# Diagonal units of stick-breaking attention: a multiply-add scan over the identity in place of two masks, and half-width products in place of zero blocks

## The chip, the cores and the metric

The kernel runs on one core of a Trainium2 chip. The metric is the device time of one execution in microseconds (us). Before the change the median of three runs is 1372.65 us (1367.76 to 1372.9). The core's engines work side by side, each through its own list of instructions in order: TensorE (PE, its weight loads apart as PEld), VectorE (DVE), ScalarE (ACT), GpSimd (POOL) and SyncE (SP), which issues the DMAs.

## The reference, cut to what matters

The model is a trunk of two layers: gated linear attention, then stick-breaking attention. Only the second concerns us, and in it the 1024 prompt tokens with 16 heads of 64 columns. Key `s` is read by query `t` only if `s < t`:

```python
z = einsum('bqhd,bkhd->bhqk', q, k) * dh ** -0.5 + bias
valid = k_pos < q_pos
log_1mb = where(valid, log_sigmoid(-z), 0.0)
rest = cumsum(log_1mb, reverse=True)          # over the keys, from the last one back
a = exp(where(valid, z + rest, -inf))
out = einsum('bhqk,bkhd->bqhd', a, v)
```

In products: with beta = sigmoid(z), the weight of key `s` is beta(s) times the product of 1 - beta over the keys from `s + 1` to `t - 1`. All arithmetic is in float32 accuracy; large products use fp32r operands, each value split into a high and a low part.

## The kernel before, in words

Layer 1 works through eight head pairs `p`. For each pair TensorE multiplies the tokens, in eight blocks `t` of 128 rows and one of 64 sample rows, by 384 columns of the input projection (q, k and v; `dense`, L293), and for every two such blocks it computes 256 tokens of the gate, transposed (`dense_t`, L315). Both write tiles called `acc`, for which there are two banks of PSUM in turn (`psum` has `bufs=2`): columns of block 2m, columns of block 2m+1, gates, columns of block 2m+2, and so on. A bank is free again once its readers are done; for columns the last reader is `qk_scale` (VectorE, L810), which waits for a power that POOL computes (`qk_sums`, L804) from a sum of squares of VectorE (L802).

Between these matmuls stand the units of attention, one for each group `m` of 256 queries, each group `c <= m` of 256 keys and each head `j` of the pair. A unit goes through four steps:

- `logits`: TensorE multiplies (L881); ScalarE makes `om` = 1 - beta (L884) and `A` = beta (L885). A tile has 512 columns: two query blocks `a` of 128 rows, 256 keys each.
- `stick`: VectorE scans `om` backwards for each query block (L908) into `run`, the running product, and multiplies `A` by `run` shifted by one key (L913 or L916). `run` goes on from the unit before by way of a small copy on POOL (L903).
- `turn`: TensorE transposes `A` (L932); ScalarE and VectorE split the result into `aT`, high (L934) and low (L935).
- `weigh`: TensorE multiplies `aT` by the values (L944), four matmuls of 256 query columns: two key blocks `x`, high and low part.

A unit with `c == m` is diagonal: there are two per group and head pair, 64 in all. In it query block 0 needs only the first 128 keys, which `logits` puts last in its half so that columns 0 to 127 of the tile stay unused. The last 128 columns of both halves hold the triangle `s < t`; there POOL sets `om` to 1 and `A` to 0 where `s >= t` (two selects, L890). Key block 1 has nothing for query block 0, so POOL fills those 128 columns of both `aT` with zeros (L926), and `weigh` multiplies them along.

The order of TensorE's work is written out: every step is given a due time (`at`), and the steps are issued in the order of these times. `PACE` is 0.42 between units, `L_STICK` 0.26, `L_TURN` 0.8 and `L_AV` 1.3 later than the logits. TensorE keeps exactly that order (`manual_schedule(engines=ENGINES)`). For the other engines a scheduler picks among the instructions that it expects to be ready, so their order can differ from the text. The weights of the next pair are split beside all this: rounded on VectorE or ScalarE (L221, L219), the rest subtracted on POOL (L222). The wait on the turned keys (`qk_p`, L853 to L859) is for `tr`, which has two banks of PSUM as well.

Of the kernel before, what the change touches and what calls it, by code (L numbers as in the profile page):

```python
# [9 lines left out]
F32 = mybir.dt.float32  # L10
F32R = mybir.dt.float32r
BF = mybir.dt.bfloat16
I32 = mybir.dt.int32
AF = mybir.ActivationFunctionType
OP = mybir.AluOpType
# [61 lines left out]
def tile_hybrid_decoder(ctx, tc, x_prompt, x_sample, state_gla, cache_k, cache_v, page_table,  # L77
# [3 lines left out]
    nc = tc.nc  # L81
# [34 lines left out]
    at = line.at  # L116
# [754 lines left out]
    def logits(u, pair, p, m, c, j):  # L871
        diag = c == m
        z = bank("z")
        k = pair["k"][c][:, j].rearrange("p (s x) -> p s x", s=2)
        mm = []
        for a in range(2):
            for q in pair["q"][m]:

                mm.append((z[:, a * 256:(a + 1) * 256], q[:, j, a * 128:(a + 1) * 128], k[:, ::-1] if diag and a == 0 else k))
        for x, (out, lhs, rhs) in enumerate(mm):  # L880
            nc.tensor.matmul(out, lhs, rhs, start=x == 0, stop=x == len(mm) - 1)  # L881
        hd, v0 = 2 * p + j, 128 if diag else 0
        u["om"], u["A"] = sb("at2", "om", [128, 512], F32, 2), sb("at2", "A", [128, 512], F32, NA)
        nc.scalar.activation(u["om"][:, v0:], z[:, v0:], AF.Sigmoid, scale=-1.0, bias=K1["bias"][:, 1, hd:hd + 1])  # L884
        nc.scalar.activation(u["A"][:, v0:], z[:, v0:], AF.Sigmoid, bias=K1["bias"][:, 0, hd:hd + 1])  # L885
        if diag:

            for x, fill in ((u["om"], 1.0), (u["A"], 0.0)):
                x = x.rearrange("p (a s) -> p a s", a=2)[:, :, 128:]
                nc.gpsimd.affine_select(x, x, pattern=[[0, 2], [-1, 128]], compare_op=OP.is_gt, fill=fill,  # L890
                                        base=0, channel_multiplier=1)

    def stick(u, pair, m, c, j):
        diag = c == m
        before = pair.get("run")
        run = pair["run"] = sb("at2", "run", [128, 2, 257], F32, 2)
        ends = (128, 256) if diag else (256, 256)
        if diag:
            for a in range(2):
                nc.gpsimd.memset(run[:, a, ends[a]:ends[a] + 1], 1.0)  # L900
        else:

            nc.gpsimd.tensor_copy(run[:, :, 256:], before[:, :, 0:1])  # L903
        for a in range(2):
            n = ends[a]
            init = 1.0 if diag else before[:, a, 0:1]
            rev = u["om"][:, a * 256 + 255:(a * 256 + 255 - n) if a * 256 + 255 - n >= 0 else None:-1]
            nc.vector.tensor_tensor_scan(run[:, a, n - 1::-1], rev, rev, init,  # L908
                                         op0=OP.mult, op1=OP.bypass)
        if diag:  # L910
            for a in range(2):
                A = u["A"][:, a * 256 + 256 - ends[a]:a * 256 + 256]
                nc.vector.tensor_mul(A, A, run[:, a, 1:ends[a] + 1])  # L913
        else:
            A = u["A"].rearrange("p (a s) -> p a s", a=2)
            nc.vector.tensor_mul(A, A, run[:, :, 1:])  # L916

    def turn(u, m, c):

        diag = c == m  # L920
        tr = psum.tile([128, 4, 128], F32, name="tr")
        hi, lo = u["aT"] = [sb("at2", f"aT{x}", [128, 512], F32R, NT) for x in range(2)]
        v0 = 128 if diag else 0
        if diag:
            for x in (hi, lo):
                nc.gpsimd.memset(x[:, :128].bitcast(F32), 0.0)  # L926
        for x in range(4):
            s, a = 1 - x // 2, x % 2
            if diag and x == 0:
                continue  # L930
            col = 128 if diag and a == 0 else a * 256 + s * 128
            nc.tensor.transpose(tr[:, x], u["A"][:, col:col + 128], ident)  # L932
        tr = tr.rearrange("p a q -> p (a q)")
        nc.scalar.activation(hi[:, v0:], tr[:, v0:], AF.Copy)  # L934
        nc.vector.tensor_sub(lo[:, v0:], tr[:, v0:], hi[:, v0:])  # L935

    def weigh(u, q, pair, c, j, first, last):
        if first:
            q["po"] = bank("o").rearrange("p (j s) -> p j s", j=2)
        n = 0  # L940
        for x in range(2):
            vs = pair["v"][c][:, 1 - x, 2 * j:2 * j + 2].rearrange("p h d -> p (h d)")
            for part in u["aT"]:
                nc.tensor.matmul(q["po"][:, j], vs, part[:, x * 256:(x + 1) * 256],  # L944
                                 start=first and n == 0, stop=last and n == 3)
                n += 1

# [31 lines left out]
    def open_at2():  # L979
        opened("at2")  # L980

        K1["turn"], K1["ql"] = 0, [sb("at2", f"ql{x}", [128, 2, 256], F32R, 1) for x in range(NQ)]
        for x in K1["ql"]:
            nc.gpsimd.memset(x.bitcast(F32), 0.0)
# [4 lines left out]
    for p in range(PAIRS):  # L989
# [27 lines left out]
        for m in range(NP // 2):  # L1017
# [10 lines left out]
            for x, (j, c) in enumerate(units):  # L1028
# [3 lines left out]
                at(z0, logits, u, pair, p, m, c, j)  # L1032
                at(z0 + L_STICK, stick, u, pair, m, c, j)
                at(z0 + L_TURN, turn, u, m, c)
                at(z0 + L_AV, weigh, u, q, pair, c, j, x == 0, x == len(units) - 1)
            at(z0 + L_AV + 0.05, gate_b, q, pair, p, m)
            at(z0 + L_AV + 0.35, store_b, q, p, m)
            if p == PAIRS - 1:
# [208 lines left out]
```

## Time and profile before

| | |
|---|---|
| Profiled execution | 1375.27 us, span 1373.6 us |
| Runs | 1372.65 us median (1367.76 to 1372.9) |
| TensorE, matmuls | 1282.8 us busy (93%), 8025 of them |
| VectorE | 1012.5 us busy (74%) |
| ScalarE | 709.7 us (52%) |
| POOL | 587.0 us (43%) |
| DMA | 115.82 MB, mean 84 GB/s |
| Chain that ended last | PE 55%, DVE 18%, POOL 9%, ACT 7%, issue 7%, DMA 3% |
| Granted TensorE clock | 0.986 of full speed over the span |

Matmuls are pipelined, and their ends are modelled: a matmul's duration includes a time in which the next one already runs, so the distance from one start to the next says more than the duration. Shares over the whole span mix three stages: layer 0 (to about 530 us), layer 1 with its attention (to about 1256 us), and the rest. A wait is named by what released it last by the profile; where the named instruction had long been done, it was another.

### The profile page before, as it was taken

The page shows a single profiled execution, that of the slowest core. Times are in us where ns is not written, and L with a number is a line of the kernel's source. Part 1 is how long each engine was busy: PE and PEld are TensorE (multiplying, and loading weights), DVE is VectorE, ACT ScalarE, POOL GpSimd, SP SyncE. Part 2 cuts the span into 40 slices and gives each one's busy share as a digit, 9 for nine tenths or more (in the row PEclk, how much of TensorE's full clock was granted, in tenths as well). Part 3 has the DMA queues.
Part 4 walks back from the last instruction along what each step waited for, and adds up shares of the span by engine and source line. Part 5 has one row for each costly group of instructions (what it writes and reads, how often), then busy time and mean ns, then how long its engine had stood idle before and what let it go on. Part 6 is the DMA issues. An engine that isn't in the chain of part 4 may idle for free.

```text
span 1373.6 us, 23656 instructions
## 1 busy us (share of the span) xinstructions
PE 1282.8 (93%) x8025; PEld 1140.3 (83%) x8025; DVE 1012.5 (74%) x2047; ACT 709.7 (52%) x1640; POOL 587.0 (43%) x1101
## 2 busy tenths in 40 slices
PE   6999999999999998989989899898998989989998
PEld 5788888888878788989889898898998988877666
DVE  7858759668564457788888988789788898986443
ACT  6446245352441134566756667566666667763221
POOL 6223223223231216465655846557466574543000
PEclk9999999999999999999999999999999999999999
DMA  6311402304246423020110201102012022134762
GB/s 195 92 32 43 137 20 68 108 32 133 91 129 213 145 101 104 18 81 18 58 42 22 79 17 55 47 24 80 16 41 63 23 89 68 32 121 155 249 245 88
DMA packets 118459, 115.82 MB, mean 84 GB/s; under 512 B 11003, under 2 KB 97923, under 8 KB 118339
## 3 DMA queue, kind: packets, MB, share of 16 engines
q1 hardware_dynamic: 118338, 114.31, 27.2%
q8 instruction: 64, 1.05, 0.3%
q14 instruction: 57, 0.46, 0.1%
HBM read 83.61 MB, written 30.67 MB: 83 GB/s over the span
## 4 chain that ended last, share of the span: by engine, by line
PE 55%; DVE 18%; POOL 9%; ACT 7%; issue 7%; DMA 3%; SPq 1%; POOLq 0%; ACTq 0%; DVEq 0%
PE acc L293 31%; PE acc L315 7%; DVE run L908 4%; PE z L881 3%; PE tr L932 3%; PE o L944 2%; POOL wlo L222 2%; POOL rs L804 2%; ACT qh L853 2%; DVE whi L221 2%; PE o L544 1%; DVE aT L935 1%; DVE wr L217 1%; POOL v L819 1%; PE o L1154 1%
## 5 line engine op out<-in xcount | busy, mean ns | idle before, releaser
L293 PE MATMUL acc<-whi,h 128*128 128x512 f32 (+1 forms) x1728 | 538.7, 374 | 10.1 <-DVE qk L810 7.9
L293 PEld LDWEIGHTS acc<-whi,h 128*128 128x128 f32 x1728 | 313.5, 189 | 41.1 <-ACT sh L954 4.2
L293 PE MATMUL acc<-wlo,h 128*128 128x512 f32 (+1 forms) x864 | 322.5, 373 | 3.9 <-DVE wlo L222 2.5
L315 PE MATMUL acc<-h,whi 128*128 128x256 f32 (+5 forms) x832 | 193.5, 318 | 10.3 <-DVE g L512 5.1
L222 POOL TENSOR_TENSOR wlo<-wr,whi 128x512 fp32r<-128x512 f32 x98 | 139.1, 1422 | 123.5 <-DVE whi L221 93.2
L293 PEld LDWEIGHTS acc<-wlo,h 128*128 128x128 f32 x864 | 162.8, 188 | 22.7 <-DVE wlo L222 3.2
L908 DVE TENSOR_TENSOR_SCAN run<-om,run 128x256 f32<-128x256 f32 x192 | 146.7, 802 | 11.0 <-ACT om L884 10.5
L315 PEld LDWEIGHTS acc<-h,whi 128*128 128x128 f32 (+2 forms) x832 | 141.3, 189 | 15.1 <-DVE g L512 6.0
L934 ACT ACTIVATE aT<-tr 128x512 fp32r<-128x512 f32 (+1 forms) x160 | 88.9, 556 | 103.9 <-PE tr L932 90.2
L884 ACT ACTIVATE om<-z,bias 128x512 f32<-128x512 f32 (+1 forms) x160 | 103.3, 646 | 52.6 <-PE z L881 43.1
L932 PE MATMUL tr<-ident,A 128*128 128x128 f32 x576 | 91.5, 277 | 39.3 <-POOL v L819 18.3
L315 PE MATMUL acc<-h,wlo 128*128 128x256 f32 (+2 forms) x392 | 123.8, 316 | 0.5 <-POOL wlo L222 0.5
L293 PE MATMUL acc<-w,h 128*128 128x384 f32 (+1 forms) x480 | 122.6, 365 | 0.7 <-DVE qk L810 0.7
L932 PEld LDWEIGHTS tr<-ident,A 128*128 128x128 f32 x576 | 69.5, 142 | 55.1 <-POOL run L903 19.4
L935 DVE TENSOR_TENSOR aT<-tr,aT 128x512 fp32r<-128x512 f32 (+1 forms) x160 | 100.8, 630 | 9.1 <-ACT aT L934 6.8
L944 PE MATMUL o<-aT,v 128*128 128x256 f32 x640 | 105.0, 286 | 0.0
L885 ACT ACTIVATE A<-z,bias 128x512 f32<-128x512 f32 (+1 forms) x160 | 102.4, 640 | 0.0
L944 PEld LDWEIGHTS o<-aT,v 128*128 128x128 f32 x640 | 97.2, 194 | 1.8 <-DVE aT L935 1.1
L908 DVE TENSOR_TENSOR_SCAN run<-om 128x128 f32<-128x128 f32 (+1 forms) x128 | 85.0, 695 | 13.6 <-POOL om L890 13.6
L881 PE MATMUL z<-kc,qh 128*128 128x256 f32 x320 | 86.1, 290 | 7.3 <-DVE kc L858 7.3
L804 POOL TENSOR_TENSOR rs<-ms,half_exp 128x4 f32<-128x4 f32 (+1 forms) x72 | 83.9, 1166 | 20.3 <-DVE ms L802 18.8
L293 PEld LDWEIGHTS acc<-w,h 128*128 128x128 f32 x480 | 82.2, 189 | 7.2 <-issue 2.5
(274 smaller groups left out, 2531.7 us busy)
## 6 DMA issues: line engine op xcount, KB each, us to landing
wr<-in_w_in_b_dram SPq DMA_DIRECT2D x64, 256.0 KB, 3.0
wr<-in_w_in_a_dram SPq DMA_DIRECT2D x32, 256.0 KB, 3.2
kp<-in_cache_k_dram SPq DMA_DIRECT2D x16, 512.0 KB, 5.0
vp<-in_cache_v_dram SPq DMA_DIRECT2D x16, 512.0 KB, 4.5
o_d<-og SPq DMA_DIRECT2D x60, 128.0 KB, 1.8
x<-in_x_prompt_dram SPq DMA_DIRECT2D x8, 512.0 KB, 4.8
wr<-in_w_in_a_dram SPq DMA_DIRECT2D x32, 128.0 KB, 3.7
n<-in_state_gla_dram SPq DMA_DIRECT2D x8, 512.0 KB, 3.9
```

The source lines that it names most:

```text
L222: engine.tensor_sub(e.lo[:, :m], raw[:, :m], e.hi[:, :m])
L293: nc.tensor.matmul(st["ps"][:x.shape[1], :n], x, (w[k].hi if part == 0 else w[k].lo)[:, :n], start=first, stop=last)
L315: nc.tensor.matmul(st[key][:x.shape[1], :n], x, y, start=first, stop=last)
L804: nc.gpsimd.tensor_tensor(st["rs"][:n], ms[:n], half_exp[:n], op=OP.pow)
L881: nc.tensor.matmul(out, lhs, rhs, start=x == 0, stop=x == len(mm) - 1)
L884: nc.scalar.activation(u["om"][:, v0:], z[:, v0:], AF.Sigmoid, scale=-1.0, bias=K1["bias"][:, 1, hd:hd + 1])
L885: nc.scalar.activation(u["A"][:, v0:], z[:, v0:], AF.Sigmoid, bias=K1["bias"][:, 0, hd:hd + 1])
L908: nc.vector.tensor_tensor_scan(run[:, a, n - 1::-1], rev, rev, init, op0=OP.mult, op1=OP.bypass)
L932: nc.tensor.transpose(tr[:, x], u["A"][:, col:col + 128], ident)
L934: nc.scalar.activation(hi[:, v0:], tr[:, v0:], AF.Copy)
L935: nc.vector.tensor_sub(lo[:, v0:], tr[:, v0:], hi[:, v0:])
L944: nc.tensor.matmul(q["po"][:, j], vs, part[:, x * 256:(x + 1) * 256], start=first and n == 0, stop=last and n == 3)
```

## The change

Three edits, all in diagonal units.

The masks go. The scan of a diagonal unit becomes state = om(s) x state + eye(s), from zero, where `eye` is 128 columns of zeros and the identity, built once when the attention opens. For `s > t` the state stays 0, at `s = t` it becomes 1, and from there it is the running product. `A` times the shifted `run` is then 0 for `s >= t` without a mask on `A`, and the first value of `run` is set to 0 in place of 1.

The zero blocks go. `weigh` multiplies key block 1 of a diagonal unit for the last 128 query columns alone, in matmuls of 128 columns in place of 256, and takes that block second, so that the first matmul of a group still writes the whole width.

The two memsets of `aT` go with them.

```diff
@@ -883,12 +883,6 @@
         u["om"], u["A"] = sb("at2", "om", [128, 512], F32, 2), sb("at2", "A", [128, 512], F32, NA)
         nc.scalar.activation(u["om"][:, v0:], z[:, v0:], AF.Sigmoid, scale=-1.0, bias=K1["bias"][:, 1, hd:hd + 1])
         nc.scalar.activation(u["A"][:, v0:], z[:, v0:], AF.Sigmoid, bias=K1["bias"][:, 0, hd:hd + 1])
-        if diag:
-
-            for x, fill in ((u["om"], 1.0), (u["A"], 0.0)):
-                x = x.rearrange("p (a s) -> p a s", a=2)[:, :, 128:]
-                nc.gpsimd.affine_select(x, x, pattern=[[0, 2], [-1, 128]], compare_op=OP.is_gt, fill=fill,
-                                        base=0, channel_multiplier=1)
 
     def stick(u, pair, m, c, j):
         diag = c == m
@@ -896,17 +890,22 @@
         run = pair["run"] = sb("at2", "run", [128, 2, 257], F32, 2)
         ends = (128, 256) if diag else (256, 256)
         if diag:
+
+
             for a in range(2):
-                nc.gpsimd.memset(run[:, a, ends[a]:ends[a] + 1], 1.0)
+                nc.gpsimd.memset(run[:, a, ends[a]:ends[a] + 1], 0.0)
         else:
 
             nc.gpsimd.tensor_copy(run[:, :, 256:], before[:, :, 0:1])
         for a in range(2):
             n = ends[a]
-            init = 1.0 if diag else before[:, a, 0:1]
             rev = u["om"][:, a * 256 + 255:(a * 256 + 255 - n) if a * 256 + 255 - n >= 0 else None:-1]
-            nc.vector.tensor_tensor_scan(run[:, a, n - 1::-1], rev, rev, init,
-                                         op0=OP.mult, op1=OP.bypass)
+            if diag:
+                nc.vector.tensor_tensor_scan(run[:, a, n - 1::-1], rev, K1["eye"][:, 255:(255 - n) if n < 256 else None:-1],
+                                             0.0, op0=OP.mult, op1=OP.add)
+            else:
+                nc.vector.tensor_tensor_scan(run[:, a, n - 1::-1], rev, rev, before[:, a, 0:1],
+                                             op0=OP.mult, op1=OP.bypass)
         if diag:
             for a in range(2):
                 A = u["A"][:, a * 256 + 256 - ends[a]:a * 256 + 256]
@@ -921,9 +920,6 @@
         tr = psum.tile([128, 4, 128], F32, name="tr")
         hi, lo = u["aT"] = [sb("at2", f"aT{x}", [128, 512], F32R, NT) for x in range(2)]
         v0 = 128 if diag else 0
-        if diag:
-            for x in (hi, lo):
-                nc.gpsimd.memset(x[:, :128].bitcast(F32), 0.0)
         for x in range(4):
             s, a = 1 - x // 2, x % 2
             if diag and x == 0:
@@ -934,14 +930,16 @@
         nc.scalar.activation(hi[:, v0:], tr[:, v0:], AF.Copy)
         nc.vector.tensor_sub(lo[:, v0:], tr[:, v0:], hi[:, v0:])
 
-    def weigh(u, q, pair, c, j, first, last):
+    def weigh(u, q, pair, m, c, j, first, last):
         if first:
             q["po"] = bank("o").rearrange("p (j s) -> p j s", j=2)
         n = 0
-        for x in range(2):
+        for x in (1, 0):
+
+            q0 = 128 if c == m and x == 0 else 0
             vs = pair["v"][c][:, 1 - x, 2 * j:2 * j + 2].rearrange("p h d -> p (h d)")
             for part in u["aT"]:
-                nc.tensor.matmul(q["po"][:, j], vs, part[:, x * 256:(x + 1) * 256],
+                nc.tensor.matmul(q["po"][:, j, q0:], vs, part[:, x * 256 + q0:(x + 1) * 256],
                                  start=first and n == 0, stop=last and n == 3)
                 n += 1
 
@@ -979,6 +977,9 @@
     def open_at2():
         opened("at2")
 
+        eye = K1["eye"] = sb("at2", "eye", [128, 256], BF, 1)
+        nc.gpsimd.memset(eye[:, :128], 0.0)
+        nc.gpsimd.tensor_copy(eye[:, 128:], identb)
         K1["turn"], K1["ql"] = 0, [sb("at2", f"ql{x}", [128, 2, 256], F32R, 1) for x in range(NQ)]
         for x in K1["ql"]:
             nc.gpsimd.memset(x.bitcast(F32), 0.0)
@@ -1032,7 +1033,7 @@
                 at(z0, logits, u, pair, p, m, c, j)
                 at(z0 + L_STICK, stick, u, pair, m, c, j)
                 at(z0 + L_TURN, turn, u, m, c)
-                at(z0 + L_AV, weigh, u, q, pair, c, j, x == 0, x == len(units) - 1)
+                at(z0 + L_AV, weigh, u, q, pair, m, c, j, x == 0, x == len(units) - 1)
             at(z0 + L_AV + 0.05, gate_b, q, pair, p, m)
             at(z0 + L_AV + 0.35, store_b, q, p, m)
             if p == PAIRS - 1:
```

The scheduler's order for ScalarE stays what it was, but for one exchange of two instructions; TensorE's is the same but for the widths. VectorE's and POOL's change. In the rows of the order, a scan is named SCALAR_TENSOR_TENSOR, a name ends in a buffer's number where one is left, and line numbers after the change are lower by a few: L904 and L907 are the scans of diagonal and other units, L912 and L915 the products (L913 and L916 before), L931 the subtraction (L935 before), L899 the copy (L903 before), L942 `weigh` (L944 before).

VectorE, third head pair, from the scaling of the sample rows on. Before:

```order
L810 TENSOR_TENSOR qk<-xr,rs_9122 64x256
L935 TENSOR_TENSOR aT_9200<-tr,aT_9199 128x512
L810 TENSOR_TENSOR qk<-acc,rs_9195 128x256
L935 TENSOR_TENSOR aT_9248<-tr,aT_9247 128x512
L908 SCALAR_TENSOR_TENSOR run<-om 128x128
L908 SCALAR_TENSOR_TENSOR run<-om 128x256
L913 TENSOR_TENSOR A<-A,run 128x128
L908 SCALAR_TENSOR_TENSOR run<-om,run 128x256
L913 TENSOR_TENSOR A<-A,run 128x256
L908 SCALAR_TENSOR_TENSOR run<-om,run 128x256
L802 TENSOR_REDUCE ms_9286<-sq 128x4
L916 TENSOR_TENSOR A<-A,run 128x512
```

The same place after the change:

```order
L810 TENSOR_TENSOR qk<-xr,rs_8995 64x256
L931 TENSOR_TENSOR aT_9071<-tr,aT_9070 128x512
L904 SCALAR_TENSOR_TENSOR run<-om,eye 128x128
L904 SCALAR_TENSOR_TENSOR run<-om,eye 128x256
L912 TENSOR_TENSOR A<-A,run 128x128
L912 TENSOR_TENSOR A<-A,run 128x256
L810 TENSOR_TENSOR qk<-acc,rs_9066 128x256
L931 TENSOR_TENSOR aT_9115<-tr,aT_9114 128x512
L907 SCALAR_TENSOR_TENSOR run<-om,run 128x256 x2
L915 TENSOR_TENSOR A<-A,run 128x512
L802 TENSOR_REDUCE ms_9153<-sq 128x4
```

The diagonal unit's four instructions have moved ahead of the scaling (L810) and of the second subtraction, and the next unit's scans behind all of these; the sum of squares (L802) has moved behind the next unit's product.

POOL, the same place, before:

```order
L804 TENSOR_TENSOR rs_9195<-ms_9190,half_exp 128x4
L812 TENSOR_TENSOR kout<-qk,kn 64x128
L222 TENSOR_TENSOR w_9098<-wr,w_9097 128x512
L890 AFFINE_SELECT om<-om 128x2x128
L890 AFFINE_SELECT A<-A 128x2x128
L820 TENSOR_TENSOR v_9276<-v,v_9276 128x128
L812 TENSOR_TENSOR kout<-qk,kn 128x128
L926 MEMSET aT_9305 128x128
L926 MEMSET aT_9306 128x128
L903 COPY run<-run 128x2
```

POOL after the change:

```order
L804 TENSOR_TENSOR rs_9066<-ms_9061,half_exp 128x4
L812 TENSOR_TENSOR kout<-qk,kn 64x128
L222 TENSOR_TENSOR w_8971<-wr,w_8970 128x512
L820 TENSOR_TENSOR v_9143<-v,v_9143 128x128
L899 COPY run<-run 128x2
L812 TENSOR_TENSOR kout<-qk,kn 128x128
```

The selects and memsets are gone; the copy of `run` has moved ahead of the product for the output (`kout`), which waits for L810.

VectorE, seventh head pair, after its diagonal scans, before:

```order
L913 TENSOR_TENSOR A<-A,run 128x128
L913 TENSOR_TENSOR A<-A,run 128x256
L908 SCALAR_TENSOR_TENSOR run<-om,run 128x256 x2
L802 TENSOR_REDUCE ms_14176<-sq 128x4
L916 TENSOR_TENSOR A<-A,run 128x512
L975 TENSOR_TENSOR h_81<-xr,h_80 128x2x256
L935 TENSOR_TENSOR aT_14196<-tr,aT_14195 128x384
L908 SCALAR_TENSOR_TENSOR run<-om,run 128x256 x2
L810 TENSOR_TENSOR qk<-acc,rs_14181 128x256
```

VectorE there after the change:

```order
L907 SCALAR_TENSOR_TENSOR run<-om,run 128x256 x2
L915 TENSOR_TENSOR A<-A,run 128x512
L802 TENSOR_REDUCE ms_13851<-sq 128x4
L973 TENSOR_TENSOR h_81<-xr,h_80 128x2x256
L931 TENSOR_TENSOR aT_13871<-tr,aT_13870 128x384
L810 TENSOR_TENSOR qk<-acc,rs_13856 128x256
L907 SCALAR_TENSOR_TENSOR run<-om,run 128x256 x2
```

The scaling (L810) has moved from behind to ahead of the last two scans.

## Rows read from the trace of the kernel before

**Rows 1.** Busy us by stretch: span, PE, PEld, DVE, ACT, POOL, PEclk, DMA, GB/s

```profile
604.00:616.00 12.00, 8.96 (x50) 8.50 (x49) 8.88 (x19) 4.06 (x9) 7.79 (x15) 0.72 0.16 44
720.00:800.00 80.00, 73.52 (x504) 70.44 (x503) 67.64 (x130) 53.85 (x116) 49.22 (x100) 0.98 0.16 46
780.00:790.00 10.00, 6.93 (x44) 6.47 (x43) 8.39 (x16) 3.71 (x9) 7.13 (x14) 0.83 0.18 49
1129.00:1140.00 11.00, 7.67 (x58) 7.03 (x57) 10.63 (x20) 6.42 (x14) 7.67 (x14) 1.00 0.28 86
```

**Rows 2.** Waits, 530 to 1256 us: who <- releaser: us, times, longest

```profile
PEld tr L932 <- POOL run L903: 19.4, 6, 3.2
...
PE tr L932 <- DVE kc L859: 11.9, 8, 1.8
...
PE acc L293 <- DVE qk L810: 8.6, 10, 1.7
...
PEld tr L932 <- POOL v L819: 1.8, 1, 1.8
```

**Rows 3.** Timeline, 776 to 789 us: start, us, engine, line, operation [idle before]

```profile
775.55 0.60 ACT L885 ACTIVATE A<-z,bias 128x384 f32<-128x384 f32 x1
...
777.42 0.67 DVE L935 TENSOR_TENSOR aT<-tr,aT 128x512 fp32r<-128x512 f32 x1
...
778.66 0.42 DVE L810 TENSOR_TENSOR qk<-acc,rs 128x256 f32<-128x256 f32 x1 [0.56 <-POOL rs L804]
...
779.00 1.28 POOL L222 TENSOR_TENSOR w<-wr,w 128x512 fp32r<-128x512 f32 x1
...
779.65 0.87 PE L315 MATMUL acc<-h,w 128*128 128x256 f32 x6
...
780.24 0.41 POOL L890 TENSOR_SCALAR_AFFINE_SELECT om<-om 128x256 f32<-128x256 f32 x1
...
780.68 1.47 DVE L908 TENSOR_TENSOR_SCAN run<-om 128x128 f32<-128x128 f32 x2 [1.01 <-POOL om L890]
...
782.08 0.47 DVE L913 TENSOR_TENSOR A<-A,run 128x128 f32<-128x128 f32 x1
...
782.47 0.77 DVE L908 TENSOR_TENSOR_SCAN run<-om,run 128x256 f32<-128x256 f32 x1
...
783.17 0.39 DVE L913 TENSOR_TENSOR A<-A,run 128x256 f32<-128x256 f32 x1
...
783.71 0.52 PE L932 MATMUL tr<-ident,A 128*128 128x128 f32 x3 [3.07 <-POOL v L819]
...
785.45 1.00 POOL L804 TENSOR_TENSOR rs<-ms,half_exp 128x4 f32<-128x4 f32 x1
...
788.54 0.52 PE L293 MATMUL acc<-w,h 128*128 128x384 f32 x2
```

**Rows 4.** Groups by form on POOL: busy us, mean ns of one | idle before

```profile
L890 POOL TENSOR_SCALAR_AFFINE_SELECT om<-om 128x256 f32<-128x256 f32 x64 | 28.2, 441 | 42.2 <-ACT om L884 42.2
```

**Rows 5.** Timeline of DVE, 711 to 713 us, a diagonal unit without subtraction beside it

```profile
711.41 1.00 DVE L908 TENSOR_TENSOR_SCAN run<-om 128x128 f32<-128x128 f32 x2
...
712.64 0.62 DVE L913 TENSOR_TENSOR A<-A,run 128x128 f32<-128x128 f32 x2
```

**Rows 6.** Timeline, 763 to 767 us, a diagonal unit beside POOL's subtraction

```profile
763.30 1.28 POOL L222 TENSOR_TENSOR wlo<-wr,whi 128x512 fp32r<-128x512 f32 x1
763.59 2.02 DVE L908 TENSOR_TENSOR_SCAN run<-om 128x128 f32<-128x128 f32 x2
```

**Rows 7.** Groups by form on DVE: layer 0's scan, multiply then add

```profile
L465 DVE TENSOR_TENSOR_SCAN t<-rst,xb 128x384 f32<-128x384 bf16 x8 | 7.5, 933 | 0.0
```

**Rows 8.** Timeline of PE, 800 to 812 us: four products of one unit

```profile
803.05 0.63 PE L944 MATMUL o<-aT,v 128*128 128x256 f32 x4
```

**Rows 9.** Groups by form on PEld: weight loads of 128 and of 32 columns

```profile
L944 PEld LDWEIGHTS o<-aT,v 128*128 128x128 f32 x640 | 97.2, 194 | 1.8 <-DVE aT L935 1.1
...
L1154 PEld LDWEIGHTS o<-vp,aTs 128*32 128x32 f32 x128 | 3.4, 115 | 4.3 <-issue 2.0 <-ACT As L1130 0.6 <-ACT oms L1129 0.4
```

## The prediction

> **What bounds the kernel now.** I began with the busy time by stretch [rows 1]. In a typical 80 us of layer 1's attention TensorE is busy 73.5 us and VectorE 67.6: TensorE sets the pace, and VectorE is close enough behind that what TensorE still loses is likely to be a wait on it. The waits of that stage [rows 2] agree: the largest single entry is six waits of 3.2 us in front of the transposes of L932, 19.4 us together; then come waits on the turned keys (L859), and on the scaling of q and k (L810) that frees an `acc` bank. Third, the order of time around one of the six [rows 3]. The reader is to see this: the sigmoids of the diagonal unit were done at 776.1, but POOL got to the select on `om` only at 780.24, behind a weight subtraction (L222), and VectorE's scans began at 780.68. VectorE had meanwhile run L810 (778.66) and another unit's subtraction, had stood idle for 1.0 us, and had the next unit's scan (782.47) between the two products. The last product ended at 783.56; the transposes started 0.15 us later, at 783.71, some 3.2 us after TensorE was ready for them (780.5). The page names POOL tiles as releasers, but those ended earlier; VectorE's L913 came last. Fourth, the clock [rows 1]: in the stretch of such a wait the granted clock is 0.83 of full speed (0.72 where the low stretch is longer), that is, some microseconds at 1.2 in place of 2.4 GHz, right after TensorE stood still. A wait of 1.8 us in the seventh pair ([rows 2], between 1129 and 1140) left the clock at 1.00.
>
> **The change, part by part.** There are 64 diagonal units, eight to a head pair.
>
> *POOL.* 128 selects go, and 128 memsets of 128 columns. The selects on `om` take 28.2 us and have 42.2 us of idle POOL ahead of them [rows 4]; those on `A` are as many and as large. POOL is not the bound, so this is worth only what it uncovers below. Added are one memset and one copy for the identity, beside dense work ahead of the attention: nothing.
>
> *The scan.* Multiply-add in place of multiply alone, with a second tensor. The trace has multiply-add scans over a bf16 and an fp32 operand: 933 ns for 384 columns [rows 7], 2.4 ns a column. The present diagonal scans, 128 and 256 columns with nothing beside them, take 1.00 us together [rows 5], 2.6 ns a column. So I take no difference. Bounds: 0.1 us less a unit, by the straight ratio; above, a second tensor could cost as much again, 1 us a unit (rival three).
>
> *Contention.* Scans beside POOL's weight subtraction took 2.02 us [rows 6] against 1.00 [rows 5]: 1.0 us more for one subtraction. The selects go, the subtractions stay.
> By the Trainium skill, "GPSIMD Engine Reference", section "Key points", POOL shares its memory interfaces with VectorE and contends with instructions that have two SBUF inputs. The two rows agree. If that gain fell on the path in all 64 units at the 1.0 us of the row, it would be 64 us; a select is shorter than a subtraction, most units have slack, and I count none of it by itself.
>
> *The order.* TensorE's order is as before but for widths. VectorE's isn't: in the block above the two scans and both products now stand together, straight behind the subtraction of 777.42, and L810 and the other subtraction behind them. Worked through with [rows 3]: the subtraction ends at 778.09; scans 1.00, products 0.62 [rows 5], and 1.0 for the L222 that starts at 779.00: `A` is ready at 780.7. L810 (0.42) ends at 781.1. That is the catch: `acc` has two banks, and the gate columns of L315, which start at 779.65, take the bank that L810 frees (it ended at 779.08, 0.57 before). With a hop of 0.15, as between 783.56 and 783.71, they now start at 781.25: a new wait of 1.6 us. The transposes stand 0.85 behind (779.65 to 780.5), so they start at 782.1 in place of 783.71: 1.6 us gained of 3.2.
>
> *What is late next.* The following L810 frees the bank of the next columns (788.54). Before it now stand a subtraction, two scans, a product and a reduction, about 0.67 + 1.5 + 0.7 + 0.4, so POOL's power (1.0) begins at 784.4 and L810 ends at 785.8, with the hop 785.95. TensorE needs 8.9 us from L315 to there, less 3.2 of wait and 1.7 of clock: it is ready at 785.25 and waits 0.7.
>
> *The clock.* (1 - 0.72) x 12 = 3.4 us, and (1 - 0.83) x 10 = 1.7. Of the six stretches two are like the first and four like the second: 13.6 us, of which about 1.1 fell on the wait itself. If 1.6 and 0.7 us apart do to the clock what 1.8 did in the seventh pair, nothing, 12.5 us come back. Bounds: 0 and 12.5.
>
> *Other waits.* L810's own, 8.6 us in ten [rows 2]: in the seventh pair L810 moves ahead of two scans; a third, 2.9. The eight on L859, 11.9 us: VectorE gets there sooner without selects beside its scans, but the subtractions stay; a fifth, 2.4. Bounds of the two together: 1 us lost in each of the eight pairs where the order goes wrong, 8, and all of the 20.5 gained.
>
> *Narrower products.* 128 matmuls go from 256 to 128 columns. Four of 256 follow each other 0.117 us apart (0.63 less the 0.28 of the last, over three) [rows 8]. Each loads its own 128 weight columns: 194 ns against 115 for 32 [rows 9], 0.82 ns a column, 105 ns for 128. I take 0.108 a matmul: 128 x 0.009 = 1.1 us. Bounds: half of 0.117, 7.5 us gained; and, as no row has fp32r under 256 columns, 0.1 us lost each, 12.8.
> The Trainium skill's "TensorE: Matmul & The Clock Gate", section "LDWEIGHTS (loading the stationary operand)", gives P/1.2 ns for P columns, 107 ns for 128: a rule against the gain. The slope of [rows 9] agrees. By it the sum has an estimate of 1.3 us here; by streaming alone, 7.5.
>
> **Sum.** Six blocks: 6 x (1.6 - 0.7) = 5.4, and 12.5 of clock. With 2.9, 2.4 and 1.1: 24.3 us. The profiled execution took 1375.3 (span 1373.6); the median of the runs is 1372.65, 2.6 lower. 1372.65 - 24.3 = 1348.4: I forecast 1348.
>
> **Rivals.**
> 1. *The bank hides* (more gain). If L222 falls elsewhere, `A` is ready at 779.7, L810 ends at 780.1, the new wait is 0.6 and the next one nil. For: POOL has less ahead of L222. Against: L222 waits for its own weights. 6 x 2.6 + 12.5 + 6.4 = 34.5: 1338.
> 2. *The wait only changes its name* (less gain). Two L222 beside the scans put L810 another 1.0 us later; 2.6 and 0.7 us of standing still bring the clock down as 3.2 did. For: [rows 6]. The six blocks then give 6 x (0.6 - 0.7), nearly nothing, and the clock nothing; 6 is left: 1367.
> 3. *The scan pays for its second operand* (slower). Twice the time is 1 us a unit, 64 in all; VectorE, at 67.6 of 80, goes over TensorE's 73.5 and becomes the bound. If three quarters land on the path, 1348 + 48 = 1396. It decides from 24 us on the path, 0.5 us a unit at that share. Against: [rows 7].
> 4. *Narrow fp32r matmuls are slow.* +12.8 on an engine that is the bound: 1361. No row speaks for it.
> 5. *It does not do what it says.* The zero columns are replaced by less work, not left for others: the order shows 128 matmuls of half width and no select in attention. I give this no chance of its own.
>
> **How the numbers follow.** Forecast 0.62, rival 1 0.13, rival 2 0.15, rival 3 0.05, rival 4 0.05. The forecast's own range is 1341 to 1357. The range of 8 in 10 takes in rivals 1 and 4, and reaches towards rival 2: 1336 to 1365. A measurement of this kernel can tell about 0.5% (7 us) from no change. The forecast, rivals 1 and 4 and a third of 2 are faster by that: 0.85; the rest of rival 2 is the same: 0.10; rival 3 is slower: 0.05.
>
> **What would show it.** Right: the 3.2 us waits at the diagonal transposes are gone, L315 waits about 1.6 us for L810 in the same six blocks, and the granted clock there is 1.00. Diagonal scans keep 1.0 us where nothing runs beside them. Narrow matmuls stand about 0.11 us apart. Wrong: clock stretches of 0.8 remain; L315's wait is over 2.5 us; scans of 256 columns over 0.8 us with POOL idle; or 0.2 us between narrow matmuls.

## The result and the profile after

The changed kernel takes 1355.18 us (1352.66 to 1355.67) against 1372.35: a ratio of 0.9884, 95% interval 0.9863 to 0.9904, or 17.2 us. A second timing, beside the first experiments, gave 1352.29 against 1371.44, 0.9859 (0.9842 to 0.9877). The forecast was 1348, with a range of 1336 to 1365. The profiled execution took 1355.22 (span 1353.5), 20.05 less than that of before.

Busy time by stretch, with the columns of [rows 1]: a typical 80 us of attention, the stretch that answers to the first of [rows 1], and one in the second head pair. The 80 us of [rows 1] were another part of attention, so the first line compares with them only roughly.

```profile
560.00:640.00 80.00, 75.06 (x524) 71.39 (x523) 68.20 (x130) 53.46 (x113) 40.57 (x69) 1.00 0.16 45
601.00:613.00 12.00, 10.06 (x72) 9.08 (x72) 11.21 (x20) 5.88 (x13) 9.65 (x14) 1.00 0.30 85
...
676.00:688.00 12.00, 9.55 (x54) 9.23 (x54) 11.39 (x20) 9.01 (x19) 8.37 (x11) 0.86 0.38 112
```

PE comes from 73.5 to 75.1 of 80 us, POOL falls from 49.2 to 40.6, and VectorE hardly moves. Where the granted clock was 0.72 it is 1.00. One low stretch has come up elsewhere, 0.86 at 676; another, at 1206, stood in the trace of before as well, at 1225.

TensorE's waits from 530 to 1240 us: who, for whom, us, times, longest.

```profile
PE acc L315 <- DVE qk L810: 9.0, 6, 1.7
PE tr L928 <- DVE kc L859: 8.3, 6, 2.4
...
PE acc L293 <- DVE qk L810: 7.1, 14, 1.2
...
PE tr L928 <- ACT A L885: 2.4, 2, 1.2
```

The six waits of 3.2 us [rows 2] are gone. L315's wait for L810, the new one of the forecast, is now the largest entry: 1.7 us in five blocks and 0.4 in the seventh pair. The last line is no new wait: it holds two of the eight that [rows 2] puts down to L859, at the same transposes. The block of [rows 3] in order of time:

```profile
772.02 1.38 POOL L804 TENSOR_TENSOR rs<-ms,half_exp 128x4 f32<-128x4 f32 x1
...
772.43 1.02 DVE L904 TENSOR_TENSOR_SCAN run<-om,eye 128x128 f32<-128x128 f32 x2
...
773.38 2.09 DVE L912 TENSOR_TENSOR A<-A,run 128x128 f32<-128x128 f32 x2
...
773.92 1.26 POOL L222 TENSOR_TENSOR w<-wr,w 128x512 fp32r<-128x512 f32 x1
...
775.39 0.41 DVE L810 TENSOR_TENSOR qk<-acc,rs 128x256 f32<-128x256 f32 x1
...
775.95 0.96 PE L315 MATMUL acc<-h,w 128*128 128x256 f32 x6 [1.72 <-DVE qk L810]
...
776.86 0.49 PE L928 MATMUL tr<-ident,A 128*128 128x128 f32 x3
...
779.98 0.42 DVE L810 TENSOR_TENSOR qk<-acc,rs 128x256 f32<-128x256 f32 x1 [0.65 <-POOL rs L804]
...
780.55 0.59 PE L293 MATMUL acc<-w,h 128*128 128x384 f32 x2 [0.23 <-DVE qk L810]
```

The scans now run early, 1.02 us, as [rows 5] had them; POOL's power (L804) stands beside them, but no subtraction. The two products, however, take 2.09, against 0.62 there: POOL's subtraction runs beside them. L810 stands behind the products and ends 0.15 before L315 starts. The transposes no longer wait at all, and the next L810 costs L293 0.23.

### The profile page after: what moved, and what is told of

Same layout as the page of the kernel before. It is cut to its first block, busy times and chain, and to the rows that moved or that the text cites. A ratio compares the mean times of both kernels' runs of the same rounds, so it can differ in the third digit from the quotient of the medians.

```text
span 1353.5 us, 23356 instructions
## 1 busy us (share of the span) xinstructions
PE 1274.4 (94%) x8025; PEld 1129.1 (83%) x8025; DVE 1008.2 (74%) x2047; ACT 708.9 (52%) x1640; POOL 516.0 (38%) x847
## 4 chain that ended last, share of the span: by engine, by line
PE 56%; DVE 23%; ACT 7%; issue 5%; POOL 4%; DMA 3%; SPq 1%; DVEq 0%; POOLq 0%; ACTq 0%
PE acc L293 33%; PE acc L315 6%; PE z L881 3%; DVE run L907 3%; PE tr L928 3%; PE o L942 2%; DVE aT L931 2%; ACT qh L853 2%; DVE whi L221 2%; POOL rs L804 2%; DVE qk L810 1%; DVE A L915 1%; DVE run L904 1%; DVE A L912 1%; PE o L544 1%
## 5 line engine op out<-in xcount | busy, mean ns | idle before, releaser
L293 PE MATMUL acc<-whi,h 128*128 128x512 f32 (+1 forms) x1728 | 540.9, 375 | 9.4 <-DVE qk L810 6.3
L293 PEld LDWEIGHTS acc<-whi,h 128*128 128x128 f32 x1728 | 313.8, 189 | 41.3 <-ACT sh L952 3.7
L293 PE MATMUL acc<-wlo,h 128*128 128x512 f32 (+1 forms) x864 | 322.9, 374 | 3.9 <-DVE wlo L222 2.6
L315 PE MATMUL acc<-h,whi 128*128 128x256 f32 (+5 forms) x832 | 191.4, 316 | 17.6 <-DVE qk L810 7.3
L222 POOL TENSOR_TENSOR wlo<-wr,whi 128x512 fp32r<-128x512 f32 x98 | 144.5, 1479 | 128.6 <-DVE whi L221 94.5
L293 PEld LDWEIGHTS acc<-wlo,h 128*128 128x128 f32 x864 | 163.1, 189 | 22.2 <-DVE wlo L222 3.2
L315 PEld LDWEIGHTS acc<-h,whi 128*128 128x128 f32 (+2 forms) x832 | 137.7, 185 | 24.4 <-issue 8.9
L907 DVE TENSOR_TENSOR_SCAN run<-om,run 128x256 f32<-128x256 f32 x192 | 142.9, 785 | 15.7 <-ACT om L884 15.1
L293 PE MATMUL acc<-w,h 128*128 128x384 f32 (+1 forms) x480 | 123.1, 366 | 0.8 <-DVE qk L810 0.8
L315 PE MATMUL acc<-h,wlo 128*128 128x256 f32 (+2 forms) x392 | 122.2, 312 | 0.3 <-POOL wlo L222 0.3
L931 DVE TENSOR_TENSOR aT<-tr,aT 128x512 fp32r<-128x512 f32 (+1 forms) x160 | 100.9, 630 | 11.1 <-ACT aT L930 8.8
L885 ACT ACTIVATE A<-z,bias 128x512 f32<-128x512 f32 (+1 forms) x160 | 102.4, 640 | 0.0
L942 PE MATMUL o<-aT,v 128*128 128x256 f32 (+1 forms) x640 | 98.8, 276 | 0.0
L942 PEld LDWEIGHTS o<-aT,v 128*128 128x128 f32 x640 | 95.2, 190 | 1.7 <-DVE aT L931 0.9
L804 POOL TENSOR_TENSOR rs<-ms,half_exp 128x4 f32<-128x4 f32 (+1 forms) x72 | 87.6, 1217 | 21.3 <-DVE ms L802 18.9
L293 PEld LDWEIGHTS acc<-w,h 128*128 128x128 f32 x480 | 82.2, 189 | 7.6 <-issue 2.9
L899 POOL COPY run<-run 128x2 f32<-128x2 f32 x96 | 32.7, 341 | 135.9 <-DVE run L907 77.5
```

The source lines that it names most:

```text
L222: engine.tensor_sub(e.lo[:, :m], raw[:, :m], e.hi[:, :m])
L293: nc.tensor.matmul(st["ps"][:x.shape[1], :n], x, (w[k].hi if part == 0 else w[k].lo)[:, :n], start=first, stop=last)
L315: nc.tensor.matmul(st[key][:x.shape[1], :n], x, y, start=first, stop=last)
L804: nc.gpsimd.tensor_tensor(st["rs"][:n], ms[:n], half_exp[:n], op=OP.pow)
L942: nc.tensor.matmul(q["po"][:, j, q0:], vs, part[:, x * 256 + q0:(x + 1) * 256], start=first and n == 0, stop=last and n == 3)
```

## The experiments

The runs stand in three sets, each timed beside the kernel before, which took 1371.44 us in the first set (the changed kernel, full width, the other sequence, the products behind L810), 1371.32 in the second (narrow products alone, idle work, the two with subtractions on VectorE) and 1372.51 in the third (no selects, six of eight on VectorE). The changed kernel itself stands only in the first, so across sets the ratios to the kernel before are compared.

> The changed kernel itself, beside the three variants of it, so that they are compared on one chip: 1355 us, with at most one low stretch of the clock inside attention.

Measured: 1352.29, ratio 0.9859, with one low stretch inside attention, again at 679.

### Which part of the change does it

First the kernel before without its selects. It leaves out the diagonal masks, and nothing stands in for them.

```diff
-            for x, fill in ((u["om"], 1.0), (u["A"], 0.0)):
-                nc.gpsimd.affine_select(...)
```

> The kernel before without its 128 selects; the diagonal masks are left out, the scans are of one tensor, the zero blocks and the full width stay. Theory A (all of the gain is the selects' going, the multiply-add scan costs nothing): 1352.5, as the changed kernel with full width, with 1.9 us in front of L315 in place of the six waits of 3.2 and no low clock there. Theory B (the second tensor costs up to 0.1 us a scan, 64 units on the path in part): 1348 to 1350. Theory C (the new scan gave part of the gain): over 1356.

Measured: 1353.96, ratio 0.9870 (0.9850 to 0.9889), against 0.9859 and 0.9884 of the changed kernel. Theory A: the selects' going gives the whole gain, as far as some 4 us of uncertainty let one tell. But VectorE's order in this run is, instruction for instruction, that of the changed kernel. So the run prices the selects together with the order that their absence brings, and doesn't part the two. In the old order of [rows 3] the scans could have started without the selects at 779.7, where VectorE fell idle, in place of 780.68: an estimate of 1.0 us for the selects by themselves. Nor was it tried to keep the selects and to move the subtraction that stands ahead of them on POOL. The largest wait is that of the changed kernel:

```profile
PE acc L315 <- DVE qk L810: 9.0, 6, 1.7
```

Then the change without the narrow products (`q0 = 0`, and the zero blocks back).

> The changed kernel with the products of the diagonal units at full width again, zero blocks and their 128 memsets on POOL included; VectorE's and ScalarE's order stay word for word. Theory A (the trace after: the second narrow product of a pair follows the first by 58 ns, and what comes next follows it by 110, in place of 117 and 118): 64 x 0.067 = 4.3 us come back, 1359.5. Theory B (the prediction: a product is bound by the load of its own weights, 0.009 us each): 1.1 us come back, 1356.3. Rival C: the memsets on POOL delay other work on the path: over 1362.

Measured: 1352.53, 0.24 more than the changed kernel. C falls. The 4.3 us of A lie at the edge of what two medians of four can tell (1350.0 to 1354.5 and 1349.5 to 1355.7), and the 1.1 of B below it, so the spacing has to decide. For theory A I had read only the products themselves. TensorE in the same unit of both, the changed kernel first, then full width:

```profile
837.78 0.57 PE L942 MATMUL o<-aT,v 128*128 128x256 f32 x4
838.19 0.39 PE L293 MATMUL acc<-whi,hs 128*128 128x384 f32 x1
838.41 0.33 PE L293 MATMUL acc<-wlo,hs 128*64 128x384 f32 x1
```

```profile
839.19 0.63 PE L944 MATMUL o<-aT,v 128*128 128x256 f32 x4
839.66 0.33 PE L293 MATMUL acc<-whi,hs 128*128 128x384 f32 x1
839.83 0.33 PE L293 MATMUL acc<-wlo,hs 128*64 128x384 f32 x1
```

The four products take 0.41 in place of 0.47 us, but the second matmul after them starts 0.22 behind the first in place of 0.17: from the first product to there it is 0.63 and 0.64. Over all 64 units 58 and 8 ns are saved at the pair and 55 are paid there: some 11 ns a unit, 0.7 us in all. A falls. A third run asks whether equal weights have a part in it.

```diff
-        for x in (1, 0):
-            for part in u["aT"]:
+        for part in u["aT"]:
+            for x in (1, 0):
```

> The changed kernel with the four products of a unit in another sequence: both blocks of the high part, then both of the low part, so that no two that follow each other have the same weights. The same products, the same widths. Theory A (58 ns apart only because the second of a pair has the weights of the first, whose load needs no wait): about 110 ns behind each narrow product, 64 x 0.052 = 3.3 us lost, 1358.5. Theory B (a narrow product takes 58 ns whatever its weights, and only the one after it waits): the narrow ones again 58 in front of what follows, or the sum of the four as in the changed kernel: 1355.

Measured: 1353.96, ratio 0.9872 (0.9856 to 0.9888), 1.7 us above the changed kernel, which two medians of four can't tell from nothing, nor from the 3.3 of theory A. The trace decides: each narrow product is followed after 58 ns by one with other weights, and the next but one comes after 170 in place of 117; the four take 407 ns (404 before). Theory A, which had 110 ns there, falls: the saving is paid back two matmuls later, whatever the weights.

And the narrow products alone, on the kernel before:

> The kernel before with only the narrow products: selects and scans as they were, no zero blocks. Its VectorE order has L810 two places earlier in six blocks. Theory (from the runs so far: 67 ns saved at the pair, 55 paid back by the second product after it, so 11 ns a unit): 0.7 us, 1371, with the six waits of 3.2 us and the low clock behind them as before. Rival (the zero blocks' memsets delay the selects on POOL): the six waits shrink below 2.5 us, 1360.

Measured: 1376.51, ratio 1.0039 (1.0020 to 1.0058): slower, and neither theory had it. The waits in front of the transposes grew from 3.1 to 3.4 us in five of six blocks, and the low clock behind them is of the long kind, 0.72 in 12 us, again in five of six blocks (one of them here, then the wait), where two had it before:

```profile
782.00:794.00 12.00, 8.61 (x48) 8.15 (x47) 9.89 (x19) 3.81 (x9) 6.79 (x12) 0.72 0.14 41
```

```profile
PE tr L929 <- DVE A L913: 21.5, 7, 3.4
```

VectorE's order moved in six places here (the L810 behind the transposes two earlier), so this run does not price the products. The longer wait arises ahead of that place. In the block of [rows 3], VectorE, then POOL:

```profile
784.13 0.90 DVE L908 TENSOR_TENSOR_SCAN run<-om,run 128x256 f32<-128x256 f32 x1
784.95 0.60 DVE L913 TENSOR_TENSOR A<-A,run 128x256 f32<-128x256 f32 x1
```

```profile
784.56 0.71 POOL L820 TENSOR_TENSOR v<-v,v 128x128 fp32r<-128x128 f32 x1
```

With the memsets gone, another subtraction of POOL (L820) comes up beside this scan and the last product. They take 0.90 and 0.60, against 0.77 and 0.39 in [rows 3], some 0.3 us together, as much as the wait has grown. That this is the cause is read from the trace, not tested, and why the clock stayed low longer was not isolated.

### The clock by itself

```diff
+        for x in range(fill):        # 16 in the six blocks
+            nc.tensor.transpose(tr[:, 0], ident, ident)
```

> The kernel before with 16 more transposes of the identity on TensorE in front of the transposes of the diagonal unit in the six blocks with a 3.2 us wait, into the block of the tr tile that nobody reads: 1.75 us of work in place of standing still, which takes nothing off the end of the wait. Theory A (the low clock follows the standing still, and about 11 of the 17 us gained are clock): the six low stretches go, 1372 - 11 = 1361, with the last transposes as late as before. Theory B (the clock falls for another reason, or the gain is all in the waits): 1372, low stretches as before.

Measured: 1362.08, ratio 0.9935 (0.9915 to 0.9955): 9.2 us gained by giving TensorE idle work. Here too the L810 behind the transposes moved a few places in the six blocks, as the addition shifts the schedule, so a small part of the 9.2 may be the order's. The block of [rows 3], and its stretch:

```profile
775.57 1.91 PE L924 MATMUL tr<-ident 128*128 128x128 f32 x16
778.79 0.52 PE L934 MATMUL tr<-ident,A 128*128 128x128 f32 x3 [1.31 <-POOL v L819]
```

```profile
772.00:784.00 12.00, 10.69 (x84) 10.07 (x83) 9.11 (x18) 4.94 (x10) 9.43 (x18) 1.00 0.23 64
```

The transposes start 3.3 us after the last matmul of the gates in front of them (775.45 to 778.79), as before, but only 1.3 of that is standing still, and the clock stays at 1.00 through all of attention. Theory A: in these blocks the low clock goes when the standing still does.

### What holds up L810

One rule for VectorE's order puts the products behind L810 in those blocks.

```diff
+                        tc.add_manual_dep(x.ins, K1["scaled"].ins.name, ...)   # product after L810
```

> The changed kernel with one rule for VectorE's order, in seven blocks (the last head pair has none): the products of the diagonal unit at the gates come behind L810, the scans stay ahead of it. Theory A (the 1.88 us in front of L315 are the wait for the bank that L810 frees; rs is there at 604.01 and the scans end at 604.06): L315's wait falls to under 0.3 us, the transposes of the diagonal unit wait about 1.0 in its place, 0.85 us gained in each of the five or six blocks that had it: 1350.5. Theory B (the wait only moves, since the products are late by as much): 1355, with waits of some 1.8 us at the transposes. Slower, if L810 has to stand idle for rs in other blocks: 1358.

Measured: 1354.37, ratio 0.9878 (0.9861 to 0.9894): nothing gained. VectorE, then POOL, then TensorE, in the first block:

```profile
603.14 0.42 DVE L810 TENSOR_TENSOR qk<-acc,rs 128x256 f32<-128x256 f32 x1
603.48 2.23 DVE L915 TENSOR_TENSOR A<-A,run 128x128 f32<-128x128 f32 x2
```

```profile
603.50 1.29 POOL L222 TENSOR_TENSOR wlo<-wr,whi 128x512 fp32r<-128x512 f32 x1
```

```profile
605.86 0.52 PE L938 MATMUL tr<-ident,A 128*128 128x128 f32 x3 [1.08 <-DVE A L915]
```

L315 no longer waits, so L810 was indeed what freed its bank. But the products, still beside the subtraction, take 2.23, the transposes wait 1.08, as theory A had it, and the next L293 waits 1.1 for its own L810, which it had left out. By the time it is theory B: the wait has moved. So the subtraction is moved instead, one a block:

```diff
+        if n in range(85, 126, 8):   # on VectorE, behind L810
+            x = nc.vector.tensor_sub(e.lo[:, :m], raw[:, :m], e.hi[:, :m])
```

> The changed kernel, with one weight subtraction (L222) a block moved from POOL to VectorE, straight behind L810, in the six blocks where it ran beside the products of the diagonal unit; VectorE's order is otherwise word for word the same. Theory A (the products take 2.1 us in place of 0.62 because of that subtraction, and with that L810 and the bank are late): products 0.62, L810 1.4 us earlier, L315's wait from 1.88 to about 0.4, some 1.5 us gained in each of five or six blocks: 1344 to 1345. Theory B (L810 waits for rs, or VectorE's 0.69 us more are lost again): 1351 to 1353.

Measured: 1346.88, ratio 0.9818 (0.9795 to 0.9841), against 0.9859 of the changed kernel: some 5.5 us less, give or take 4.

```profile
603.26 0.86 DVE L921 TENSOR_TENSOR A<-A,run 128x128 f32<-128x128 f32 x2
604.04 0.41 DVE L817 TENSOR_TENSOR qk<-acc,rs 128x256 f32<-128x256 f32 x1
604.37 0.68 DVE L224 TENSOR_TENSOR wlo<-wr,whi 128x512 fp32r<-128x512 f32 x1
```

```profile
604.60 0.47 PE L322 MATMUL acc<-h,whi 128*128 128x256 f32 x2 [0.47 <-DVE qk L817]
...
609.80 0.41 PE L300 MATMUL acc<-whi,h 128*128 128x384 f32 x1 [0.83 <-DVE qk L817]
```

The products are down from 2.09 to 0.86, by as much as the subtraction takes on POOL, and L315's wait (L322 here) from 1.7 to 0.47; 0.6 of the 1.25 goes to the next L810. So the mechanism was that of theory A, but not its sum. From start to start of TensorE, between this trace and that of the changed kernel in the first set, 5.5 us are gained in front of L315 and 3.4 lost in front of L293, 2.1 in all. Another 2.8 come from the second pair, where a wait of 2.4 us and the low clock behind it are gone; they are gone in the run with the products behind L810 too, which moved no subtraction. What happens there stands under *The clock* below. Then all 64 of them (`engine` is VectorE there):

> The changed kernel with all 64 weight subtractions of the attention stage on VectorE in place of POOL. Theory A (a subtraction beside VectorE's scans and products holds them up by 1.0 to 1.5 us, more than the 0.69 us that it takes on VectorE): waits shrink in most blocks, 1342 to 1350. Theory B (VectorE, 74% busy, takes 44 us more and becomes the bound, since most subtractions now run beside PSUM reads that they do not hold up): 1360 to 1375.

Measured: 1346.16, ratio 0.9815 (0.9792 to 0.9837): inside the times of theory A, but no different from the run before it (1343.3 to 1346.9 here, 1343.9 to 1348.3 there). The other 58 subtractions bring nothing more that the times can tell. Attention in the changed kernel and in this one:

```profile
560.00:1240.00 680.00, 637.68 (x4374) 603.51 (x4373) 589.92 (x1127) 454.32 (x962) 337.43 (x573) 1.00 0.18 55
```

```profile
560.00:1240.00 680.00, 640.70 (x4414) 606.24 (x4413) 590.24 (x1198) 456.45 (x967) 265.47 (x511) 1.00 0.19 58
```

In the same 680 us VectorE does 71 instructions more, 64 of them these subtractions, in the same busy time, 590 us: what it takes over is paid for by what no longer holds it up. L315's wait for L810 is gone. But a new wait has come: two subtractions now stand together in front of one product.

```profile
PE tr L928 <- DVE A L915: 13.0, 8, 2.2
```

The last of this line puts those two back on POOL.

> The run before it with the subtractions on VectorE, but the two of each head pair that stood together on VectorE in front of a product (1.4 to 1.7 us of new wait in seven pairs) back on POOL: six of eight a pair on VectorE. Theory A (the new wait was VectorE's own 1.26 us for those two): the new wait goes and the rest stays, 1346 - 8 = 1338. Theory B (on POOL the two hold up the scan and the product beside them by as much, as they did in the changed kernel): the wait there is again that of the changed kernel, 1342 to 1346.

Measured: 1361.7, ratio 0.9920 (0.9899 to 0.9940). Both theories missed. The order changed with the engines: the second L810 of a block is now behind two scans, and in three blocks L293 waits 1.9 to 2.0 for it. The wait that was to go has grown, from 13.0 to 15.0 us, and the low clock is back four times, each time right behind one of these waits (1.9, 2.0, 1.9 and 2.3 us at 856, 942, 1028 and 1202). That the order is the cause was not tested by itself.

```profile
PE acc L293 <- DVE qk L810: 15.0, 16, 2.0
PE tr L928 <- DVE A L915: 15.0, 8, 2.3
```

## Why the prediction was right, and where its sizes were off

Direction, range and mechanism held; the gain was over-sized, 24.3 forecast and 17.2 measured. TensorE's 8025 matmuls stand in the same order in both traces, so the difference can be worked out start by start. In the six blocks the intervals in front of L315, of the transposes and of the next L293 are counted. Elsewhere in attention an interval counts as a wait where TensorE stood idle before the matmul in one of the traces, else as clock where the granted clock was low, else as narrower products from the first product of a diagonal unit to the second matmul behind its four:

| us | forecast | between the two profiles |
|---|---|---|
| waits of the six blocks | 5.4 | 8.1 |
| clock | 12.5 | 9.4 |
| other waits (L810, L859) | 5.3 | 4.5 |
| narrower products | 1.1 | 0.6 |
| rest of attention | 0 | -1.8 |
| outside attention | 0 | -0.7 |
| sum | 24.3 | 20.05 |

*Six blocks.* The transposes gained 19.3 us, L315 lost 9.4, together 9.9 against the 9.6 of six times 1.6; the next L293 lost 1.8 in place of six times 0.7. The new wait of 1.6 us at L315 came as 1.7 in five blocks, the 0.7 at the next L293 as 0.2 to 0.6. That the 1.6 came out so well is partly luck: the 1.0 us of POOL's subtraction was put on the scans. They kept 1.02, and the products took it, with 1.5. The price of 1.0 was itself read too simply: beside the scans of [rows 6] there stood a select on `A` (764.53) and the start of another L222 (765.04) as well.

*The clock.* Of the terms, this step was the most over-sized. "12.5 us come back" took the upper bound itself. The low stretches of the six blocks did return 10.9, but a new one took 1.5. It came in the second head pair, where the two scans of another diagonal unit met two subtractions in a row and its second product a third (POOL, VectorE, then TensorE):

```profile
672.96 1.27 POOL L222 TENSOR_TENSOR wlo<-wr,whi 128x512 fp32r<-128x512 f32 x1 [0.42 <-DVE whi L221]
674.18 1.41 POOL L222 TENSOR_TENSOR w<-wr,w 128x512 fp32r<-128x512 f32 x1
...
676.35 1.29 POOL L222 TENSOR_TENSOR w<-wr,w 128x512 fp32r<-128x512 f32 x1
```

```profile
672.73 0.68 DVE L931 TENSOR_TENSOR aT<-tr,aT 128x512 fp32r<-128x512 f32 x1
673.34 2.81 DVE L904 TENSOR_TENSOR_SCAN run<-om,eye 128x128 f32<-128x128 f32 x2
...
676.60 1.32 DVE L912 TENSOR_TENSOR A<-A,run 128x256 f32<-128x256 f32 x1 [0.28 <-POOL run L899]
```

```profile
679.83 0.52 PE L928 MATMUL tr<-ident,A 128*128 128x128 f32 x3 [2.45 <-DVE kc L859]
```

The scans take 2.81 us, the second product starts 0.28 late, by the profile behind POOL's copy of `run` (L899), and takes 1.32; the turned keys are late, TensorE stands for 2.5 us, and the clock falls right after. The scans alone don't do it. In the third pair of the same trace they take as long, but there the products get in ahead of the third subtraction, which starts at 760.96:

```profile
757.94 2.81 DVE L904 TENSOR_TENSOR_SCAN run<-om,eye 128x128 f32<-128x128 f32 x2
760.67 0.60 DVE L912 TENSOR_TENSOR A<-A,run 128x128 f32<-128x128 f32 x2
```

The wait there is 1.2 us and the clock stays at 1.00. The second pair shows both cases. All five traces with the changed kernel's order on VectorE (the two of the changed kernel, no selects, full width, the other sequence) have the held product, a wait of 2.4 to 2.6 us and the low stretch. The run with the products behind L810 and the one with six subtractions on VectorE have the same scans of 2.81, but products of 0.6, waits of 1.3 and 1.2, and no low stretch.

The forecast rested on a wait of 1.8 us in the seventh pair that left the clock at 1.00, and the 1.7 us waits at L315 cost no clock in this execution either; in one of the experiments, that with alternating weights, one of them did. The trace of before had shown as much, and I overlooked it:

```profile
1223.77 0.50 PE L293 MATMUL acc<-whi,h 128*128 128x512 f32 x1 [1.56 <-DVE xr L725]
```

Behind this wait, in the last pair, the granted clock was 0.86 from 1221 to 1233.

*The base.* 2.9 us of the miss are none of the terms. The profiled execution of before lay 2.9 above the median of its runs, and I took the full sum of its terms off that median. Of the clock, too, I had one execution's count; the run with idle work, which has no low stretch left in attention, puts it at some 9.2 by medians.

*Scan.* No difference, as taken: 1.02 against 1.00. *Other waits.* L810's outside the six blocks, with the seventh pair's transposes, gave 3.0 from start to start, as forecast (2.9). L859's eight gave 1.1 against 2.4. Its line falls from 11.9 to 8.3, but two of the eight, 2.4 us, stand in the line of ScalarE's L885 after the change, and one has grown into the long wait of the second pair. *Narrower products.* 11 ns a unit against the 18 that two at 0.009 make; and the sign, 0.11 us apart, held for one of two, since the other was followed after 58 ns. The rule of the Trainium skill that I set against the gain ("TensorE: Matmul & The Clock Gate", "LDWEIGHTS (loading the stationary operand)") comes nearer to the measured 0.7 us, with its estimate of 1.3, than streaming alone, with 7.5; that the load is what bounds these products was not tested. *Rest.* The -1.8 and -0.7 were put at nothing, and what makes them up was not followed.

*Rivals.* Rivals 2 to 4 fell: the clock came back, the scan costs nothing more, and narrow products lose nothing. Rival 1 held in one of the six blocks, that of the second pair: the subtraction starts after the products there, these take 0.60, and L315 does not wait (VectorE, then POOL).

```profile
689.17 0.60 DVE L912 TENSOR_TENSOR A<-A,run 128x128 f32<-128x128 f32 x2
689.69 0.42 DVE L810 TENSOR_TENSOR qk<-acc,rs 128x256 f32<-128x256 f32 x1
```

```profile
690.06 1.29 POOL L222 TENSOR_TENSOR wlo<-wr,whi 128x512 fp32r<-128x512 f32 x1
```

## What to carry to other kernels

Where another engine's queue stands in a short chain that the bound engine waits for, remove that step before making any step shorter: here the selects, which stood behind a 1.3 us subtraction, were with the order that hung on them all of the gain. Price what comes next on each engine of the chain beside what runs there, and ask of a helper engine what it holds up, not how busy it is. Moving six of 64 subtractions gave all that moving the 64 gave, as far as the times can tell. Take a clock's loss from several executions, at less than its full size, since a change that ends one long wait may leave another. And follow a wait by its place in the order, not by the name of what released it: a name can change while the wait stays.

## What the runs showed of the hardware

- POOL's subtraction of two SBUF tensors (1.3 us for 128x512) held up VectorE's scans and products with two SBUF operands in every block shown: two products of 0.62 us took 2.09 beside one and 0.86 with it moved away, and two scans of 1.02 took 2.81 beside two. The Trainium skill's "GPSIMD Engine Reference", section "Key points", names the contention; the price, more than the 0.68 of doing the work on VectorE, is from these runs. Not each instruction of POOL did it: the scans of 772.43 took 1.02 with POOL's power (L804, 128x4) beside them nearly to their end. A subtraction on VectorE that reads PSUM was not held up. This one, before the change, stands wholly beside the L222 of [rows 3] and takes the 0.67 to 0.68 us that it takes elsewhere:

```profile
779.00 0.68 DVE L935 TENSOR_TENSOR aT<-tr,aT 128x512 fp32r<-128x512 f32 x1
```

- A short matmul's saving can be gone two matmuls later: 58 ns were saved at a narrow product, 55 lost at the second one after the pair.
- In the attention stage of the twelve traces (530 to 1240 us) a low clock followed all 12 waits of over 3.1 us, 13 of 58 between 1.7 and 3.1, and none of some 170 between 1.0 and 1.7 (from start to start of TensorE's matmuls, less the 0.17 of one of 384 columns); there was no low clock without such a wait. The same wait in the same place had it in one execution and not in another: that of L293 in the last pair (1.5 us idle, 1.7 by this count) in the trace after the change, but not in the repeat of the changed kernel. What else decides there stays open.
